# The identity held in the factor of the DeltaNet's solves: one VectorE operation for each Newton residual

## The chip, the cores and the metric

One Trainium2 chip, one core of it. The metric is the device time of one launch in microseconds (us); the figures compared are medians of several launches. TensorE (PE in the profile, PEld its weight loads), VectorE (DVE), ScalarE (ACT), GpSimd (POOL) and the DMA queues of SyncE (SP) each work through a list of instructions in order, and wait for one another by semaphores.

## The reference

One decoder layer for 512 tokens of width 1024: norm, an input projection whose columns feed three groups of heads, an output projection, and an MLP. Only the gated DeltaNet (6 heads of 64, chunks of 64 tokens) bears on the change:

```python
decay = jnp.exp(jnp.where(causal, gc[..., :, None] - gc[..., None, :], -jnp.inf))
L = jnp.where(strict, jnp.einsum('bhncd,bhnsd->bhncs', k_beta, k) * decay, 0.0)
A = jnp.eye(C, dtype=f32) + L
u = lax.linalg.triangular_solve(A, v * beta[..., None], left_side=True, lower=True, unit_diagonal=True)
w = lax.linalg.triangular_solve(A, k_beta * jnp.exp(gc)[..., None], left_side=True, lower=True, unit_diagonal=True)
...
def step(S, xs):
    v_new = u_i - jnp.einsum('bhcd,bhde->bhce', w_i, S)
    o = jnp.einsum('bhcd,bhde->bhce', qd_i, S) + jnp.einsum('bhcs,bhse->bhce', qk_i, v_new)
    S = S * gl_i[..., None, None] + jnp.einsum('bhcd,bhce->bhde', kd_i, v_new)
    return S, o
```

## The kernel before

The kernel inverts A = I + L for each chunk. Tokens lie in 4 tiles of 128 (two chunks each), and `gdn_solve(i)` does tile i for all six heads at once: a 128x384 tile holds six 64x64 blocks on each half of the partitions, and `sysmm` (its matmuls are all on L809) multiplies them block by block, 12 steps of two 64x64 matmuls.

A solve first doubles an approximate inverse in float16 (T16 and its transpose TT16, six rounds on L834 to L846), then corrects it by Newton steps in float32. X is the approximation (a copy of T16, made by GpSimd on L857). `residual()` forms r = I - X - L X: IX = I - X on L852, and R = IX - L X on L854, where L X is a product in PSUM of the transposed factor LT and X. Then X += T r (L860), the transpose TT1 is corrected the same way (L863), a second residual follows, and the last correction (L870) is written over LT as d["TT"], the inverse's transpose. L874 multiplies it with k. `gdn_prep_k` makes LT (`decayed`, L755) and its negative float16 copy L16 (L777).

The solves run two by two: tiles 0 and 1, then 2 and 3 (`solves`). `gdn_step` (L889, L893, L897, L906, L909, L914) is one step of the scan over chunks; its steps 4 to 8 need the second pair of solves. `gdn_out` (L928 to L938) normalizes a tile's outputs. All of that shares the engines with the input projections of the other heads (`proj_tok`, L434: 128x256 matmuls against hi and lo halves of the weights; L559 and L547 belong to the key and query heads that these projections feed, L148 and L683 copy their results out), with the compression MLP (`compress_half`, L597, L608, L639), and behind the last projection with the attention (L1072 to L1149) and the output projection (L142 to L144 on the tiles hwo, lwo). A projection of `proj_tok` holds two of three PSUM banks (pm), so its second half waits until the projection before has been read out of the bank that it takes over.

The order on each engine isn't written by hand. `side_by_side` interleaves generators, and then a scheduler places all instructions by its own model of their times: the context is opened with `schedule_with_timeline_sim=True`. So a change of a few instructions can move many others.

Of the kernel before, what the change touches and what calls it, by code (L numbers as in the profile page):

```python
# [16 lines left out]
ALU = mybir.AluOpType  # L17
# [4 lines left out]
T = 512  # L22
# [15 lines left out]
def trunk_kernel(ctx, tc, x, norm_mix, w_in, conv_w, a_log, dt_bias, gdn_norm, nsa_q_norm, nsa_k_norm,  # L38
                 cmp_pos, cmp_w1, cmp_w2, pool_w, pool_scale, w_out, norm_ffn, w_ffn1, w_ffn2, out):
    nc = tc.nc  # L40
    V, S, G, PE, SY = nc.vector, nc.scalar, nc.gpsimd, nc.tensor, nc.sync
# [31 lines left out]
    def ctile(shape, dt, name):  # L73
        return cst.tile(shape, dt, tag=name, name=name)
# [201 lines left out]
    id2 = ctile([P, 64], F32, "id2")  # L276
# [4 lines left out]
    for p in range(2):  # L281
        h = slice(64 * p, 64 * p + 64)
# [84 lines left out]
    for m in range(6):  # L367
        n = 1 << m
        G.memset(lvf[:, m], 0.0)
        for p in range(2):  # L370
            h = slice(64 * p, 64 * p + 64)
# [5 lines left out]
    for p in range(2):  # L377
        h = slice(64 * p, 64 * p + 64)
# [337 lines left out]
    gt = gte.enter_context(pool("gt", 1))  # L716
    GB = dict(kT=2, D1=2, LT=4, QK=4, qdT=4, tmp=3, gls=2, vn=2, S=3, L16=4)
    for a in range(2):
        GB.update({f"X{a}": 1, f"IX{a}": 1, f"TT1{a}": 1, f"T{a}": 4, f"R{a}": 2})

    def bch(r):
        return r.unsqueeze(2).to_broadcast([P, H, HD])
# [1 line left out]
    def bs(m):  # L724
        return m.unsqueeze(1).to_broadcast([P, 6, 64])

    def w1t(shape, name, tag=None, dt=F32):
        tag = tag or name
        pl_ = gs if tag in ("LT", "QK", "qdT", "gls", "vn", "S", "tmp") else gt
        return pl_.tile(shape, dt, tag=tag, name=nm(name), bufs=GB[tag])  # L730

    def hcol(s_):

        return 2 * (s_ % 3) + s_ // 3

    def v6(ps):
        return ps[:, 0:384].rearrange("p (s c) -> p s c", s=6)

    def head_T(src):

        ps = pp_()
        for j in range(3):
            PE.transpose(ps[:, ts(j, P)], src[:, 2 * j:2 * j + 2, :].rearrange("p a d -> p (a d)"), ident)
        return ps[:, 0:384].rearrange("p (j a t) -> p j a t", j=3, a=2)

    def decayed(dst, kT, qT, dec):

        for hp in range(2):
            kk = pp_()
            for j in range(3):  # L750
                for p in range(2):
                    PE.matmul(kk[halves[p], ts(j, 64)], kT[halves[hp], j, p], qT[halves[hp], j, p], start=True, stop=True)
            yield 0.3
            ss = slice(3 * hp, 3 * hp + 3)
            V.tensor_tensor(dst[:, ss], kk[:, 0:192].rearrange("p (s c) -> p s c", s=3), dec[:, ss], ALU.mult)  # L755

    def gdn_prep_k(i):

        gU = w1t([P, 2, 3, 64], "gU", "tmp")
        gi = g[:, i].rearrange("p (j a) -> p a j", a=2)  # L760
        for hp in range(2):
            G.tensor_tensor(gU[:, hp], gi[:, hp].unsqueeze(2).to_broadcast([P, 3, 64]),
                            le64.unsqueeze(1).to_broadcast([P, 3, 64]), ALU.mult)
        de = pp_()
        PE.matmul(de[:, 0:384], sgt, gU.rearrange("p a j c -> p (a j c)"), start=True, stop=False, skip_group_check=True)
        PE.matmul(de[:, 0:384], identb, bs(nm64), start=False, stop=True, skip_group_check=True)
        yield 0.9
        D1, LT = w1t([P, 6, 64], "D1"), w1t([P, 6, 64], "LT")
        D0 = w1t([P, 6, 64], "D0", "tmp")
        S.activation(D1, v6(de), AF.Exp)  # L770
        V.tensor_tensor(D0, D1, bs(lt64), ALU.mult)
        kT = w1t([P, 3, 2, 64], "kT")
        S.copy(kT, head_T(kr[:, i]))
        yield 0.4
        yield from decayed(LT, kT, kT, D0)
        L16 = w1t([P, 6, 64], "L16", "L16", F16)
        V.tensor_scalar(L16, LT, -1.0, None, ALU.mult)  # L777
        grp[i] = dict(kT=kT, D1=D1, LT=LT, L16=L16)
        have.add(("k", i))

# [23 lines left out]
    def sysmm(pb, lhsT, rhs):  # L804

        ps = pb()
        for s_ in range(6):
            for p in range(2):
                PE.matmul(ps[halves[p], ts(s_, 64)], lhsT(halves[p], s_), rhs(halves[p], s_), start=True, stop=True)  # L809
        return v6(ps)  # L810

    def at(t):
        return lambda h, s_: t[h, s_]
# [8 lines left out]
    def gdn_solve(i):  # L822


        d = grp[i]
        LT = d["LT"]
        ln = i % 2
        pb = (pga, pgb)[ln]

        def tl(name, tag, dt=F32):  # L830
            return w1t([P, 6, 64], name, f"{tag}{ln}", dt)

        T16, TT16 = WI[ln][0], WI[ln][6]
        V.copy_predicated(TT16, bs(lv[:, 6]), d["L16"])  # L834
        for m in range(6):
            W = WI[ln][m]
            yp = sysmm(pb, at(d["L16"]), (lambda h, s_: id16[h]) if m == 0 else at(T16))
            V.copy_predicated(W, bs(lv[:, m]), yp)
            yield 0.33
            if m:  # L840
                nt = tl("T16", "T", F16)
                S.copy(nt, sysmm(pb, at(TT16), at(W)))
                yield 0.33
                tt = tl("TT16", "T", F16)
                S.copy(tt, sysmm(pb, at(W), at(TT16)))
                T16, TT16 = nt, tt  # L846
                yield 0.33

        X, IX = tl("X", "X"), tl("IX", "IX")

        def residual():
            V.tensor_tensor(IX, bs(id2), X, ALU.subtract)  # L852
            r = tl("R", "R", F16)
            V.tensor_tensor(r, IX, sysmm(pb, lambda h, s_: LT[h, s_], at(X)), ALU.subtract)  # L854
            return r

        G.tensor_copy(X, T16)  # L857
        r = residual()
        yield 0.8
        V.tensor_tensor(X, sysmm(pb, at(TT16), at(r)), X, ALU.add)  # L860
        yield 0.33
        TT1 = tl("TT1", "TT1")
        V.tensor_tensor(TT1, sysmm(pb, at(r), at(TT16)), TT16, ALU.add)  # L863
        t16 = tl("TT16", "T", F16)
        S.copy(t16, TT1)
        yield 0.33
        r = residual()
        yield 0.8
        d["TT"] = LT
        V.tensor_tensor(d["TT"], sysmm(pb, at(r), at(t16)), TT1, ALU.add)  # L870
        yield 0.33
        yield from until(("q", i))
        ke = kr[:, i]
        S.mul(ke, sysmm(pb, lambda h, s_: ke[h, hcol(s_)], at(d["TT"])), -1.0)  # L874
        yield 0.8
# [120 lines left out]
    def until(*names):  # L996
        while not have.issuperset(names):
            yield -1
# [11 lines left out]
    def solves():  # L1010
        for i in range(2):
            yield from gdn_prep_k(i)
        for ab in ((0, 1), (2, 3)):
            yield from until(*(("k", i) for i in ab))
            yield from in_turn(gdn_solve(i) for i in ab)
            have.add(ab)

    def preps():
        yield from until("q")
        for i in range(4):  # L1020
            if i == 2:
                yield from gdn_prep_k(2)
                yield from gdn_prep_k(3)
            yield from gdn_prep_q(i)
# [314 lines left out]
    for e in range(NE):  # L1339
# [40 lines left out]
        X, Y, Z = (0, 1), (2, 3), (6, 7)  # L1380
# [45 lines left out]
```

## Time and profile before

| what | value |
|---|---|
| median of 3 runs | 719.96 us (719.61 to 721.62) |
| the profiled execution's own time | 720.69 us |
| its span, first to last instruction | 718.7 us |
| PE busy | 695.0 us (97%) |
| DVE busy | 554.6 us (77%) |
| ACT busy | 385.0 us (54%) |
| POOL busy | 170.2 us (24%) |
| granted TensorE clock, mean | 0.997 of full |

Busy times are of single engines and overlap. [...] In rows of single instructions the first two numbers are the start and the duration in us, x counts instructions, and brackets give the idle time before the first of them with what ended it.

### The profile page before, as it was taken

The numbers are of one execution on the slowest core, as the hardware profiler recorded it, in microseconds if no ns is written. First come the engines' busy times: TensorE is split into PE (matmuls) and PEld (weight loads), VectorE is DVE, ScalarE is ACT, GpSimd is POOL, SyncE is SP. The second block draws the span as 40 slices with busy tenths as digits, with TensorE's granted clock in tenths as the row PEclk, the third lists the DMA queues.
The fourth block names the chain that finished last, engine by engine and source line by source line (L and its number), as shares of the span: only waits on it lengthen the run. The fifth ranks groups of instructions, "written<-read, shape, count | busy, mean of one in ns | idle before, by whom it ended". The sixth has DMA issues, their size and how long they took to land.

```text
span 718.7 us, 13300 instructions
## 1 busy us (share of the span) xinstructions
PE 695.0 (97%) x5161; PEld 570.1 (79%) x5161; DVE 554.6 (77%) x1041; ACT 385.0 (54%) x768; POOL 170.2 (24%) x257
## 2 busy tenths in 40 slices
PE   8999999999979898999889999999999999999997
PEld 7888777888969776676679878888888888888885
DVE  6688998888786669877454997977968686796836
ACT  5465845665744558686643845444544544634430
POOL 6820023313112400000030330504032140504123
PEclk9999999999999999999999999999999999999999
DMA  6343213142301503220120153333051423312103
GB/s 223 97 132 88 76 44 90 31 119 65 105 3 32 234 2 93 85 87 2 59 88 2 59 176 127 108 102 132 10 167 59 131 103 118 118 36 85 57 0 117
DMA packets 49923, 62.20 MB, mean 87 GB/s; under 512 B 5495, under 2 KB 42565, under 8 KB 49861
## 3 DMA queue, kind: packets, MB, share of 16 engines
q1 hardware_dynamic: 48996, 61.16, 27.0%
q8 instruction: 40, 0.66, 0.4%
q10 hardware_dynamic: 864, 0.20, 0.1%
q14 instruction: 23, 0.18, 0.1%
HBM read 59.25 MB, written 2.10 MB: 85 GB/s over the span
## 4 chain that ended last, share of the span: by engine, by line
PE 80%; DVE 10%; ACT 3%; DMA 3%; issue 2%; POOL 0%; SPq 0%; DVEq 0%; ACTq 0%; POOLq 0%
PE ps L142 19%; PE ps L143 18%; PE ps L144 18%; PE ps L434 7%; PE ps L809 3%; PE ps L1149 2%; PE ps L260 2%; PE ps L597 1%; PE ps L1135 1%; DMA raw<-in_w_in_dram 1%; ACT P L1116 1%; DMA raw<-in_cmp_w_dram 1%; DVE lw L134 1%; DVE bl L1302 1%; PE ps L1110 1%
## 5 line engine op out<-in xcount | busy, mean ns | idle before, releaser
L143 PE MATMUL ps<-h2l,hw 128*128 128x512 f32 (+1 forms) x280 | 104.9, 375 | 0.2 <-DVE h2l L1273 0.2
L144 PE MATMUL ps<-h2h,lw 128*128 128x512 f32 (+1 forms) x280 | 104.5, 374 | 0.0
L142 PE MATMUL ps<-h2h,hw 128*128 128x512 f32 (+1 forms) x280 | 103.8, 374 | 0.0
L1309 POOL TENSOR_TENSOR al<-gF,ah 128x512 fp32r<-128x512 f32 x24 | 36.4, 1516 | 224.0 <-ACT ah L1308 184.6
L142 PE MATMUL ps<-bh,ah 128*128 128x512 f32 x224 | 88.4, 395 | 0.7 <-DVE x L1395 0.7
L143 PE MATMUL ps<-bl,ah 128*128 128x512 f32 x224 | 88.1, 393 | 0.0
L144 PE MATMUL ps<-bh,al 128*128 128x512 f32 x224 | 84.5, 393 | 0.0
L1395 DVE TENSOR_TENSOR x<-ps,x 128x512 f32<-128x512 f32 x112 | 72.7, 680 | 8.4 <-PE ps L144 8.4
L1302 DVE TENSOR_TENSOR bl<-w2r,bh 128x1024 fp32r<-128x1024 f32 x40 | 57.8, 1446 | 6.6 <-ACT bh L1301 6.6
L143 PEld LDWEIGHTS ps<-h2l,hw 128*128 128x128 f32 x280 | 52.6, 188 | 10.4 <-DVE h2l L1273 0.4
L144 PEld LDWEIGHTS ps<-h2h,lw 128*128 128x128 f32 x280 | 52.6, 188 | 10.0
L142 PEld LDWEIGHTS ps<-h2h,hw 128*128 128x128 f32 x280 | 52.3, 188 | 10.1
L1309 POOL TENSOR_TENSOR al<-gS,ah 128x512 fp32r<-128x512 f32 x32 | 53.8, 1698 | 22.1 <-ACT ah L1308 22.1
L1301 ACT CAST bh<-w2r 128x1024 fp32r<-128x1024 f32 x40 | 41.8, 1047 | 26.5 <-PE ps L144 26.0
L134 DVE TENSOR_TENSOR lo<-raw,hi 128x512 fp32r<-128x512 f32 (+1 forms) x76 | 43.0, 587 | 11.0 <-ACT hi L133 10.4
L133 ACT CAST hi<-raw 128x512 fp32r<-128x512 f32 (+1 forms) x76 | 37.4, 518 | 26.2 <-DMA raw<-in_w_in_dram 9.5
L142 PEld LDWEIGHTS ps<-bh,ah 128*128 128x128 f32 x224 | 42.1, 188 | 11.4 <-ACT ah L1308 0.9
L144 PEld LDWEIGHTS ps<-bh,al 128*128 128x128 f32 x224 | 42.1, 188 | 9.8
L143 PEld LDWEIGHTS ps<-bl,ah 128*128 128x128 f32 x224 | 42.1, 188 | 9.6
L134 DVE TENSOR_TENSOR lw<-raw,hw 128x1024 fp32r<-128x1024 f32 x32 | 41.2, 1321 | 5.8 <-ACT hw L133 5.7
L133 ACT CAST hw<-raw 128x1024 fp32r<-128x1024 f32 x32 | 32.2, 1046 | 25.0 <-PE ps L143 22.7
L1308 ACT CAST ah<-gS 128x512 fp32r<-128x512 f32 x32 | 19.7, 621 | 46.4 <-DVE gS L1377 24.4
(370 smaller groups left out, 1676.8 us busy)
## 6 DMA issues: line engine op xcount, KB each, us to landing
raw<-in_w_ffn_dram SPq DMA_DIRECT2D x32, 512.0 KB, 3.9
w2r<-in_w_ffn_dram SPq DMA_DIRECT2D x32, 512.0 KB, 4.6
raw<-in_w_in_dram SPq DMA_DIRECT2D x24, 256.0 KB, 3.0
raw<-in_w_in_dram SPq DMA_DIRECT2D x36, 128.0 KB, 2.5
x<-in_x_dram SPq DMA_DIRECT2D x8, 512.0 KB, 6.2
raw<-in_cmp_w_dram SPq DMA_DIRECT2D x32, 128.0 KB, 2.8
raw<-in_w_out_dram SPq DMA_DIRECT2D x8, 512.0 KB, 4.3
out_dram<-x SPq DMA_DIRECT2D x8, 256.0 KB, 2.0
```

What stands on the lines that cost most here:

```text
L133: {"A": S.copy, "V": V.tensor_copy, "G": G.tensor_copy}[e[0]](hi[:, k], r)
L134: {"V": V, "G": G}[e[1]].tensor_tensor(lo[:, k], r, f32v(hi[:, k]), ALU.subtract)
L142: PE.matmul(ps, ah, bh, start=start, stop=False, **kw)
L143: PE.matmul(ps, ah, bl, start=False, stop=False, **kw)
L144: PE.matmul(ps, al, bh, start=False, stop=stop, **kw)
L434: PE.matmul(ps[:, ts(i, 256)], a_[:, k, ts(2 * b + i, P)], w_, start=(k == 0 and n_ == 0 and i == 0), stop=(k == KC - 1 and n_ == 2 and i ...
L809: PE.matmul(ps[halves[p], ts(s_, 64)], lhsT(halves[p], s_), rhs(halves[p], s_), start=True, stop=True)
L1301: S.copy(hi, src)
L1302: V.tensor_tensor(lo, src, f32v(hi), ALU.subtract)
L1308: S.copy(hi, src)
L1309: G.tensor_tensor(lo, src, f32v(hi), ALU.subtract)
L1395: V.tensor_tensor(x2[i][:, cs], acc[bk, t_], x2[i][:, cs], ALU.add)
```

## The change

L852 and the tile IX go. In their place the identity id2 (a 64x64 identity in each block, read as a broadcast) is added to LT once for each tile, in `gdn_prep_k` behind L777, where L16 has already been taken from it. LT's diagonal was zero, so LT then holds the transpose of I + L, and the product in PSUM is X + L X; R = id2 - that product is one operation. The two IX tiles (128x384 float32, one for each of the pair) are no longer allocated. The product's matmuls are the same in number and shape.

```diff
-        GB.update({f"X{a}": 1, f"IX{a}": 1, f"TT1{a}": 1, f"T{a}": 4, f"R{a}": 2})
+        GB.update({f"X{a}": 1, f"TT1{a}": 1, f"T{a}": 4, f"R{a}": 2})
...
         L16 = w1t([P, 6, 64], "L16", "L16", F16)
         V.tensor_scalar(L16, LT, -1.0, None, ALU.mult)
+        V.tensor_tensor(LT, LT, bs(id2), ALU.add)
         grp[i] = dict(kT=kT, D1=D1, LT=LT, L16=L16)
...
-        X, IX = tl("X", "X"), tl("IX", "IX")
+        X = tl("X", "X")

         def residual():
-            V.tensor_tensor(IX, bs(id2), X, ALU.subtract)
             r = tl("R", "R", F16)
-            V.tensor_tensor(r, IX, sysmm(pb, lambda h, s_: LT[h, s_], at(X)), ALU.subtract)
+            V.tensor_tensor(r, bs(id2), sysmm(pb, lambda h, s_: LT[h, s_], at(X)), ALU.subtract)
             return r
```

On every engine the instructions are the same but for those on DVE (8 of L852 gone, 4 additions new), yet their order differs from the middle of the first solves on. In the changed program lines from 778 to 850 stand one higher (L809 is L810 there). The pieces below show three places.

**VectorE, the Newton steps of the second pair.** X_2785 and X_2815 before, X_2783 and X_2811 now, belong to tiles 2 and 3; R, IX and TT1 (shown as TT) likewise. qks, r and rs belong to a norm of the key heads, and ps_3824 before, ps_3816 now, is the bank that the second half of the next projection takes over when L547 has read it. Before:

```order
L852 TENSOR_TENSOR IX_2816<-id_148,X_2815 128x384
L111 SCALAR_TENSOR_TENSOR r_4016<-rs_4021,r_4016 128x4
L863 TENSOR_TENSOR TT_2908<-ps_2909,TT_2767 128x384
L547 TENSOR_TENSOR qks_4014<-ps_3824,r_4016 128x2x128
L854 TENSOR_TENSOR R_2929<-IX_2786,ps_2930 128x384
```

and in the changed program:

```order
L547 TENSOR_TENSOR qks_4006<-ps_3816,r_4008 128x2x128
L613 SCALAR_TENSOR_TENSOR hh_3960<-ht_3961,hh_3960 128x128
L839 COPY_PREDICATED W_570<-lv,ps_2656 128x384
...
L854 TENSOR_TENSOR R_2785<-id_148,ps_2786 128x384
L111 SCALAR_TENSOR_TENSOR r_4032<-rs_4037,r_4032 128x4
...
L860 TENSOR_TENSOR X_2783<-ps_2831,X_2783 128x384
```

L547, which releases the bank, stood behind seven operations of the Newton steps on X, R and TT and four on IX; now it stands ahead of all of them.

**TensorE, the same place.** L809 and L810 are the solves' products, L434 the projection into the bank named above (ps_4085 before, ps_4077 now). Before:

```order
L809 MATMUL ps_2790<-X_2785,LT_1375 64x64 x12
...
L639 MATMUL ps_2707<-w_3962,hh_3968 32x64 x12
L809 MATMUL ps_2820<-X_2815,LT_1410 64x64 x12
...
L809 MATMUL ps_2837<-R_2789,TT_2749 64x64
...
L809 MATMUL ps_2930<-X_2785,LT_1375 64x64 x12
L809 MATMUL ps_2949<-X_2815,LT_1410 64x64 x12
L434 MATMUL ps_4085<-hi_4086,hTh 128x256
```

and in the changed program:

```order
L810 MATMUL ps_2786<-X_2783,LT_1377 64x64 x12
L559 MATMUL ps_4054<-ident,X_4002 128x128
...
L434 MATMUL ps_4077<-hi_4078,hTl 128x256
...
L810 MATMUL ps_2831<-R_2785,TT_2747 64x64
L434 MATMUL ps_4077<-lo_4079,hTh 128x256
...
L810 MATMUL ps_2814<-X_2811,LT_1413 64x64 x12
L810 MATMUL ps_2878<-TT_2747,R_2785 64x64
```

Before, from the first residual's product to the second residuals' products no projection stands between them, only the 12 rows of L639; now 11 rows of L434 stand between the first residual's product and the next product of the solves (TT16 with W), and 21 between the first correction and the residual of the other tile, and such runs go on to the end of the solves.

**TensorE, the end of the projections.** L434 is the last projection, L1072 the first of the attention, L889 and L914 steps of the scan (ps_3327 is step 6 before; ps_3239 and ps_3279 are steps 4 and 5 now). Before:

```order
L434 MATMUL ps_4224<-hi_4283,hTl 128x256
L1072 MATMUL ps_4513<-KCT,XT_3564 128x64 x2
L1072 MATMUL ps_4513<-KCT,XT_3571 128x64 x4
L889 MATMUL ps_3327<-vb,LT_1410 64x64
L889 MATMUL ps_3327<-vb,LT_1375 64x64
```

and in the changed program:

```order
L434 MATMUL ps_4216<-hi_4275,hTl 128x256
L1072 MATMUL ps_4505<-KCT,XT_3556 128x64
L914 MATMUL ps_3239<-S_3209,qdT_1450 64x64
...
L1072 MATMUL ps_4505<-KCT,XT_3563 128x64 x4
L1072 MATMUL ps_4496<-KCT,XT_3549 128x64 x4
L1072 MATMUL ps_4496<-KCT,XT_3556 128x64 x2
L889 MATMUL ps_3279<-vb,LT_1377 64x64 x6
```

Of the steps that need the second pair, 4 and 5 stood ahead of the projections' end before; now the end of step 4 and all of 5 to 8 stand behind it, among the attention. On VectorE's list L932 of the last tile moves from place 590 to 609; on TensorE's the fourth L936 stands 17 rows ahead of the third head's L1170, 33 before. Behind the middle of the attention the orders on TensorE have met again.

## Rows read from the trace of the kernel before

**Rows 1.** The page: busy time of the engines.

```profile
PE 695.0 (97%) x5161; PEld 570.1 (79%) x5161; DVE 554.6 (77%) x1041; ACT 385.0 (54%) x768; POOL 170.2 (24%) x257
```

**Rows 2.** Windows: busy time by stage (x instructions), granted clock, DMA.

```profile
core 0: us, PE busy (x) PEld busy (x) DVE busy (x) ACT busy (x) POOL busy (x), PEclk, DMA share, GB/s
150.00:170.00 20.00, 19.68 (x404) 17.15 (x402) 16.68 (x50) 11.78 (x32) 2.17 (x5) 1.00 0.32 94
199.80:209.62 9.82, 6.09 (x181) 5.20 (x174) 8.82 (x30) 4.45 (x17) 1.01 (x2) 1.00 0.01 2
209.62:213.30 3.68, 3.68 (x53) 3.56 (x54) 2.57 (x8) 1.88 (x5) 1.74 (x4) 0.54 0.00 0
213.30:238.70 25.40, 25.40 (x341) 23.82 (x341) 14.96 (x43) 9.35 (x22) 7.73 (x15) 1.00 0.08 23
238.70:250.00 11.30, 9.06 (x119) 6.95 (x118) 9.78 (x29) 8.19 (x21) 4.21 (x7) 1.00 0.86 334
250.00:275.00 25.00, 25.00 (x181) 19.01 (x180) 18.76 (x51) 14.67 (x39) 1.02 (x1) 1.00 0.06 20
275.00:300.00 25.00, 21.95 (x126) 15.80 (x124) 23.50 (x67) 20.67 (x56) 1.01 (x1) 1.00 0.34 109
```

**Rows 3.** Timeline of PE, the end of the second pair.

```profile
202.35 0.92 PE L809 MATMUL ps<-X,LT 64*64 64x64 f32 x24 [0.41 <-ACT TT L845]
...
203.38 1.14 PE L639 MATMUL ps<-w,hh 128*32 128x64 f32 x24
204.96 0.92 PE L809 MATMUL ps<-X,LT 64*64 64x64 f32 x24 [0.44 <-ACT TT L845]
...
207.41 0.38 PE L809 MATMUL ps<-R,TT 64*64 64x64 f16 x12 [1.34 <-DVE R L854]
...
209.08 0.38 PE L809 MATMUL ps<-TT,R 64*64 64x64 f16 x12 [0.76 <-DVE X L860]
209.62 2.71 PE L809 MATMUL ps<-X,LT 64*64 64x64 f32 x48 [0.16 <-DVE TT L863]
...
216.42 1.61 PE L809 MATMUL ps<-LT,kr 64*64 64x64 f32 x48
```

**Rows 4.** Timeline of DVE, the same stretch.

```profile
205.08 0.54 DVE L852 TENSOR_TENSOR IX<-id,X 128x384 f32<-128x384 f32 x1
...
205.93 0.17 DVE L103 TENSOR_SCALAR r<-ss 128x4 int32<-128x4 int32 x1
...
206.81 0.55 DVE L854 TENSOR_TENSOR R<-IX,ps 128x384 f16<-128x384 f32 x1
...
207.93 0.56 DVE L852 TENSOR_TENSOR IX<-id,X 128x384 f32<-128x384 f32 x1
...
210.49 0.41 DVE L547 TENSOR_TENSOR qks<-ps,r 128x256 f32<-128x256 f32 x1
```

**Rows 5.** Lines L852 and L771: durations (ns min/median/max).

```profile
L852 DVE TENSOR_TENSOR IX<-id,X x8: 541/548/557, 146.6 to 209.5; 128x384 f32<-128x384 f32 x8
L771 DVE TENSOR_TENSOR D<-D,lt x4: 546/554/559, 55.8 to 127.3; 128x384 f32<-128x384 f32 x4
```

**Rows 6.** The chain that ended last: one run of projections.

```profile
225.61 3.19 PE ps L434 x25
```

**Rows 7.** Lines on PE, 238.7 to 300 us, by what was waited for.

```profile
L1110 PE MATMUL ps<-XT,XT 128*128 128x256 f32 (+3 forms) x28 | 10.3, 367 | 2.3 <-ACT P L1116 2.3
...
L1095 PE MATMUL ps<-ident,pc 128*96 128x128 f32 x4 | 0.6, 282 | 1.1 <-DVE pc L1091 1.1
```

**Rows 8.** Timeline: the last tile of the scan and of gdn_out.

```profile
270.43 0.54 DVE L929 TENSOR_REDUCE ss<-sq 128x6 f32<-128x384 f32 x1
285.65 0.55 DVE L932 TENSOR_TENSOR vb<-vb,r 128x384 f32<-128x384 f32 x1
...
286.34 1.01 POOL L933 TENSOR_TENSOR vb<-vb,zt 128x384 f32<-128x384 f32 x1 [32.30 <-DVE vb L932]
...
295.16 0.52 PE L936 MATMUL ps<-ident,vb 128*128 128x128 f32 x3 [0.18 <-DVE yTl L148]
```

## The prediction

> **What bounds the kernel now.** The page's first part comes first: PE is busy 695.0 of 718.7 us, DVE 554.6 [rows 1]. PE leaves 718.7 - 695.0 = 23.7 us idle in the whole span, and no edit on DVE can gain more than PE's idle time plus what PE loses to a low clock. So the second view is the windows, to see where near the change PE is idle or slow [rows 2]. The first pair's Newton steps lie in 150 to 170 us, under projections and compression: PE is busy 19.68 of 20.00 us there. The second pair's end is different. From 199.80 to 209.62 us PE is busy 6.09 of 9.82, so 3.73 us are idle, and from 209.62 to 213.30 it is busy throughout but at a granted clock of 0.54, which is nearly all of it at the lower of its two levels. Then PE is full to 238.7 us. In the attention 2.24 us of 11.30 and 3.05 of 25.00 are idle again.
>
> The third view is the timeline of PE in the poor stretch [rows 3]. Nothing but the solves' own small products and the compression's last ones (L639) stands there. The longest wait is 1.34 us for R of L854, another is 0.76 us for X of L860. The timeline of DVE shows why those are late [rows 4]: DVE is busy 8.82 of the 9.82 us [rows 2] and works off its queue in order. Between IX at 205.08 and R at 206.81 stand the first steps of a small rsqrt chain (L103 at 205.93 and on); IX at 207.93 stands directly behind the first tile's X and in front of the second's. The projection that could fill PE needs a bank that L547 frees, and L547 runs only at 210.49, behind all of that. So the hole is made by two queues that are interleaved badly, not by the Newton steps' length alone.
>
> **The change part by part.**
>
> *Operations.* Eight IX operations of 0.548 us go, four additions come; L771 is the nearest row for them (float32, same shape, one operand a broadcast): 0.554 us [rows 5]. DVE saves 8 x 0.548 - 4 x 0.554 = 2.17 us. R reads the broadcast identity where it read IX; L852 itself reads that broadcast at 0.548, so I take no change for R. The additions stand in front of the four solves' first mask operation (L834) and delay each by 0.55 us, at a time when PE has other work; without that cover it would be 4 x 0.55 = 2.2 us. On PE no instruction is added or removed. If nothing moved, the direct gain would be the IX operations on the chain of the poor stretch: four of them, 2.2 us, of which the part that turns into PE's waiting is at most the waits behind them (R 1.34, X 0.76 and the 0.16 before TT1's product [rows 3] give about 2.1).
>
> *The order.* This is the larger part, and it is told from the pieces of the two lists in the section on the change. L547 now stands in front of the second pair's residuals on DVE, so the bank is free, and PE's list has 11 and 21 projections between the products that waited for R and X. In a plain run 25 of them take 3.19 us on the chain that ended last [rows 6], 0.128 each, so 11 are 1.4 us and 21 are 2.7 us of cover. What must be covered is one DVE operation of 0.55 us and what is queued in front of it, which was 1.26 us at the first R of the poor stretch (205.55, where IX gave DVE free, to 206.81). So most of the 3.73 us should go.
>
> *The clock.* With the hole goes the slow stretch behind it: at a clock of 0.54, 3.68 us do the work of 3.68 x 0.54 = 1.99 us, so 1.69 us are lost. A direct check: 48 float32 products of 64x64 take 2.71 us at 209.62, and the same number at 216.42, at full clock, takes 1.61 [rows 3]; that alone is 1.10 us. [...]
>
> *What stays.* The new order also has two tight places: two products in a row that both need fresh masks (W) from DVE, and the last residual of tile 3. The first pair's stretch, which is covered in the same manner, still idles 20.00 - 19.68 = 0.32 us for two tiles' Newton steps [rows 2]. The bounds of what stays are 0 and the whole 3.73; I take 0.7, twice that row, since the new order's runs of projections are broken into more pieces than a plain one.
>
> *The attention.* The end of step 4 and steps 5 to 8 of the scan now stand among the attention instead of 4 and 5 ahead of it. PE's work is only moved. It can fill idle time there (5.29 us between 238.7 and 300 [rows 2], mostly waits for exponentials of L1116, 2.3 us, and for L1091, 1.1 us [rows 7]), or make DVE and ACT later, since DVE is busy 23.50 of the 25.00 us from 275 on [rows 2]. DVE's share of what is moved is small: about two steps of two operations, none longer than a 128x384 operation, so at most 4 x 0.55 = 2.2 us, as much as the change saves on DVE. I take 0, with bounds of 2 us either way, the idle time of 238.7 to 250 on the one side and those 2.2 us on the other.
>
> *The sum.* -3.73 - 1.69 + 0.7 + 0 = -4.7 us against the profiled execution: 720.69 - 4.7 = 716.0. That execution lies 0.73 us above the median, so against 719.96 it is 715.3 us.
>
> **The rivals.**
>
> *No change.* The hole is filled but the time isn't kept: either PE still waits (for masks, or for the DVE queue, which now has four residues of weights, L134, to do between the Newton steps), or the attention gives it back. For it speaks that DVE is nearly full in both stretches, 8.82 of 9.82 and 23.50 of 25.00 us. Against it: DVE is busy only 14.96 of 25.40 us in between [rows 2], and this is the stretch that the solves' end now shares. [...] The time by this rival: 719.96, within 2.2 either way.
>
> *Only the direct gain.* The new order brings nothing, and only the IX operations on the chain count, with the slow clock staying: 719.96 - 2.1 = 717.9. It lies on the border of what can be told apart.
>
> *Slower: the scan's end becomes late.* The last tile's `gdn_out` takes 270.43 to 285.65 on DVE, because its small operations are queued among the softmax's, then GpSimd until 287.35, and PE transposes the result at 295.16: 7.8 us of slack [rows 8]. In the new order the last scan step stands later against the attention, and on DVE the last L932 comes 19 places further down, while PE's last transpose moves by 16 of PE's rows only. At 23.50 us for 67 operations, 0.35 us each [rows 2], that is 6.7 us: the slack is nearly used up. If queueing is worse than this mean, PE stops at that transpose with the attention queued behind it. It turns the sign when that wait exceeds the 4.7 us gained, which is from 7.8 + 4.7 = 12.5 us of delay on. With each of the 19 places at twice the mean the delay is 13.3 us, and if in steps 5 to 8 of the scan each of two DVE operations is held up by one more of the mean, 4 x 2 x 0.35 = 2.8 us come to it: 13.3 + 2.8 - 7.8 = 8.3 us of waiting, and 719.96 + 8.3 - 4.7 = 723.6. That needs all of it to be late at once.
>
> **How the numbers follow.** A measurement of this kernel tells differences of about 0.3%, 2.2 us, from none. The forecast with its own spread has 0.66; the direct gain alone 0.08, half of it below the border; no change 0.16; slower 0.10. That gives faster 0.70, same 0.20, slower 0.10. The likeliest case's own range is 712.5 (all of 5.42 gained, and 2 more in the attention) to 717.8. The range for 8 in 10 goes up into the no-change case: 712.3 to 720.3, which leaves out the upper half of no change and the slower case above, and a little below.
>
> **What would show it.** In the changed kernel's windows the stretch between the compression's last product and the last projection should show PE busy in more than 95% and a clock of 1.00; the waits for R and X should be under 0.5 us together; the last projection should end some 7 to 8 us earlier than 238.7, because of the 4.7 us and of the scan's products that went behind it; the fourth L936 should wait less than 1 us. From 300 us on all stages should be equal, moved by one offset. I am wrong if PE's waits for DVE at the solves remain above 2 us, if the clock still falls there, or if the transposes of `gdn_out` or L1110 wait longer than before by as much as was gained.

## The result: 1.15% slower

The changed kernel takes 728.92 us (727.08 to 730.33, 4 runs) beside 719.97 (719.61 to 721.62, 4 runs) for the kernel before: the ratio is 1.0115, 95% interval 1.0098 to 1.0133. Its profiled execution took 727.69 us, with a span of 725.9, 7.2 more than that of before. The medians lie 8.95 us apart, the two profiled executions 7.0: the changed kernel's two longer executions (730.16 and 730.33) had a mean granted clock of 0.988 and 0.986, the two shorter ones 0.991. The prediction, 715.3 with a range up to 720.3, is wrong, and on the other side.

The page's first part, beside [rows 1]:

```profile
PE 700.5 (97%) x5161; PEld 574.2 (79%) x5161; DVE 554.7 (76%) x1037; ACT 384.9 (53%) x768; POOL 171.0 (24%) x257
```

VectorE's busy time is that of before, and PE is 5.5 us longer busy with the same 5161 products. In the changed kernel's trace the projections' products (L434, 128x256) are 415 to 452 ns long on the mean from 178.2 to 183.4 us, at a granted clock of 0.50, and 286 to 289 from 184 to 236 us, at 1.00, so this points at the clock. The windows, beside [rows 2]:

```profile
150.00:170.00 20.00, 19.72 (x404) 17.01 (x401) 16.77 (x50) 13.30 (x36) 2.19 (x5) 1.00 0.40 110
170.00:175.00 5.00, 4.11 (x98) 3.54 (x98) 4.72 (x22) 1.78 (x6) 1.64 (x4) 1.00 0.02 6
175.00:178.17 3.17, 0.44 (x20) 0.33 (x16) 1.69 (x4) 1.24 (x4) 2.17 (x5) 0.80 0.00 0
178.17:184.00 5.83, 5.83 (x56) 5.13 (x56) 1.38 (x3) 3.77 (x10) 0.65 (x1) 0.52 0.19 46
204.00:236.50 32.50, 31.92 (x522) 30.04 (x522) 19.31 (x54) 12.64 (x33) 11.25 (x20) 1.00 0.07 19
236.50:250.00 13.50, 12.70 (x156) 10.10 (x155) 11.94 (x38) 9.41 (x26) 3.29 (x4) 1.00 0.80 312
250.00:275.00 25.00, 25.00 (x230) 19.40 (x229) 19.17 (x57) 15.19 (x41) 3.29 (x4) 1.00 0.00 1
275.00:300.00 25.00, 20.49 (x113) 14.79 (x111) 22.37 (x68) 18.75 (x50) 2.05 (x1) 0.93 0.27 85
```

The poor stretch at the second pair's end is gone: from 204 us to the last projection PE is busy 31.92 of 32.50 us at full clock. But at the second pair's *start* there is a new one: 175 to 178.17 us has 0.44 us of work, and the 5.83 us behind it run at a clock of 0.52. (In slices of 0.2 us the clock of both traces is 1.00 or 0.50, but for 2 slices of before and 6 of the changed kernel at the edges of slow stretches.) The timeline of PE shows the wait:

```profile
173.74 0.38 PE L810 MATMUL ps<-W,TT 64*64 64x64 f16 x12 [0.90 <-DVE W L839]
...
175.04 0.40 PE L810 MATMUL ps<-T,L 64*64 64x64 f16 x10
178.17 0.53 PE L810 MATMUL ps<-TT,W 64*64 64x64 f16 x12 [2.73 <-ACT T L843]
178.63 0.58 PE L597 MATMUL ps<-hi,fs 128*128 128x256 f32 x1
```

PE waits 2.73 us for T of L843. ScalarE's timeline shows what that stands behind:

```profile
172.93 0.47 ACT L846 CAST TT<-ps 128x384 f16<-128x384 f32 x1
176.93 0.81 ACT L554 CAST X<-qks 128x256 fp32r<-128x256 f32 x2 [3.53 <-POOL qks L550]
177.65 0.47 ACT L843 CAST T<-ps 128x384 f16<-128x384 f32 x1
178.02 0.27 ACT L633 CAST KCT<-ps 128x128 fp32r<-128x128 f32 x1
```

The casts of L554 wait 3.53 us for GpSimd's qks (L550), which needs L547 from VectorE, and VectorE reaches that only at the end of a chain of small operations:

```profile
175.00 0.17 DVE L111 SCALAR_TENSOR_TENSOR r<-rs,r 128x8 f32<-128x8 f32 x1
175.20 0.37 DVE L546 TENSOR_SCALAR r<-r 128x4 f32<-128x4 f32 x1
175.60 0.69 DVE L547 TENSOR_TENSOR qks<-ps,r 128x512 f32<-128x512 f32 x1
176.21 0.55 DVE L839 CAST_PREDICATED W<-lv,ps 128x384 f16<-128x384 uint16 x1
```

It is the picture of [rows 4] again, a small rsqrt chain and L547 among the solves' work, 30 us earlier and with ScalarE's queue as the second link. What covered this stretch before were projections. The rows of L434 alone, of before and then of the changed kernel:

```profile
170.00:190.00 20.00, 9.31 (x67) 8.19 (x65) 1.00 0.41 106
190.00:210.00 20.00, 3.65 (x24) 3.13 (x24) 0.99 0.06 17
```

```profile
170.00:190.00 20.00, 5.70 (x31) 4.70 (x29) 0.83 0.24 61
190.00:210.00 20.00, 10.58 (x72) 9.39 (x73) 1.00 0.22 62
```

From 170 to 190 us 31 projections run where 67 did, and from 190 to 210 us 72 where 24 did: the cover of the old hole is missing at the new one.

Two windows for each kernel divide the 7 us: 60 us to the attention's first product (L1072), and from there to the first L1268, the first product behind the attention. Of before, then of the changed kernel:

```profile
60.00:238.70 178.70, 173.55 (x2514) 150.19 (x2512) 147.81 (x395) 102.12 (x250) 38.69 (x60) 0.99 0.24 63
238.70:370.16 131.46, 121.65 (x752) 89.15 (x750) 97.89 (x244) 85.99 (x213) 10.24 (x22) 1.00 0.22 77
```

```profile
60.00:236.50 176.50, 171.25 (x2428) 148.05 (x2427) 143.78 (x376) 100.46 (x245) 37.06 (x59) 0.98 0.24 64
236.50:377.13 140.63, 128.44 (x836) 94.64 (x834) 100.41 (x259) 87.85 (x218) 12.65 (x22) 0.98 0.21 72
281.50:287.00 5.50, 5.12 (x21) 3.65 (x21) 5.05 (x16) 5.17 (x16) 0.00 (x0) 0.69 0.29 97
361.00:366.00 5.00, 4.97 (x14) 3.50 (x15) 1.39 (x2) 1.19 (x2) 0.00 (x0) 0.66 0.00 0
```

| | idle PE, before and after | lost to the clock | length without both |
|---|---|---|---|
| to L1072 | 5.15 and 5.25 | 1.69 and 2.80 | 171.86 and 168.45 |
| attention | 9.81 and 12.19 | 0 and 3.41 | 121.65 and 125.03 |

Idle time is length less busy time. The clock's loss is the length of each slow stretch times what its clock lacks, where PE is busy: 5.83 x 0.48 = 2.80 behind the new hole (the lower clock in the hole itself falls on time that is already counted as idle), and 5.50 x 0.31 + 5.00 x 0.34 = 3.41 at 281.5 and 361 us. The last column shows the scan's products that moved (86 fewer rows in the first window, 84 more in the second). The differences are +0.10 +1.11 -3.41 and +2.38 +3.41 +3.38. The moved work cancels, and 6.97 us are left, 4.52 of them the clock's and 2.48 idle time. From there on both kernels run alike (offset 6.97 at L1268, 7.2 at the end).

### The profile page after: what moved, and what is told of

Its sections match the earlier page's. It is cut to its first block, busy times and chain, and to the rows that moved or that the text cites. A ratio compares the mean times of both kernels' runs of the same rounds, so it can differ in the third digit from the quotient of the medians.

```text
span 725.9 us, 13295 instructions
## 1 busy us (share of the span) xinstructions
PE 700.5 (97%) x5161; PEld 574.2 (79%) x5161; DVE 554.7 (76%) x1037; ACT 384.9 (53%) x768; POOL 171.0 (24%) x257
## 4 chain that ended last, share of the span: by engine, by line
PE 80%; DVE 9%; ACT 5%; DMA 3%; issue 2%; SPq 0%; POOL 0%; DVEq 0%; ACTq 0%; POOLq 0%
PE ps L143 19%; PE ps L142 19%; PE ps L144 19%; PE ps L434 6%; PE ps L810 3%; PE ps L597 2%; PE ps L260 2%; PE ps L1149 2%; DMA raw<-in_w_ffn_dram 2%; DMA raw<-in_w_in_dram 1%; PE ps L1135 1%; PE ps L1110 1%; DVE lw L134 1%; ACT P L1116 1%; PE ps L1268 1%
```

## Experiments

Two theories. **Order**: the scheduler's new order of the queues makes the time, and the operations little of it. **Work**: the operations themselves (additions ahead of the solves, a residual that reads a broadcast) cost it. Where an experiment holds an order, its kernel gets this function and a table of each engine's instructions, which is called behind the kernel's body:

```diff
+def _follow(tc, nc, order):
...
+    for e, text in order.items():
...
+        row = [per[e][k] for k in struct.unpack(f"<{len(raw) // 2}H", raw)]
+        for a, b in zip(row, row[1:]):
+            tc.add_manual_dep(b, a.name, nosync, reason="order")
```

No kernel was run with its own order held, so what holding costs by itself isn't measured. That it is little is argued from the fifth experiment, which is held and still faster than before.

**First and second: operations and order crossed.** The new operations in the old order, and the old ones in the new order.

> The changed kernel's operations, with every engine's queue held in the order of the kernel before; each addition stands directly behind the negation of L777, and nothing is left out. If the order decides, this is the time of before less what the missing IX operations gave on the chain: 717.9 to 720.0 us, with the hole of 199.8 to 209.6 us shortened by at most 2.1. If the operations themselves decide (the additions ahead of the solves' first masks, the residual's broadcast operand), it is near the changed kernel's 728.9.

> The operations of the kernel before (IX in, no additions), with every engine's queue held in the order of the changed kernel; each IX stands directly ahead of its residual. If the order decides, this is the changed kernel's time plus at most the eight IX operations: 728.9 to 731. If the operations decide, it is near 720.

Measured: 723.37 us for the first, 1.0024 of before (1.0009 to 1.0040), and 727.71 for the second, 1.0086 (1.0070 to 1.0103), with 721.04 for before beside them. With the old operations the new order loses 0.86% of the changed kernel's 1.15%, and its trace has the same wait of 2.7 us for T. So the order is most of the loss, though the time lies 1.2 us below the range that this theory had; the rest, 0.29%, is at the edge of the two intervals and not explained. But the first was not the small gain that the order theory wanted: by its ratio it lost 1.7 us. Its trace shows where, ScalarE's and then PE's rows:

```profile
115.51 0.62 ACT L133 CAST hi<-raw 128x512 fp32r<-128x512 f32 x1 [3.58 <-DMA raw<-in_w_in_dram]
```

```profile
117.35 1.82 PE L671 MATMUL ps<-pM,PW 128*128 128x512 f32 x2 [2.43 <-issue]
```

A weight's transfer is late: its cast starts at 115.51, in the fifth experiment at 113.23. Its residue on VectorE follows at 116.38, behind that the pooling's last L668 at 117.09, and PE's L671 waits 2.43 us and starts right after it (the view names no releaser). Two additions stand at 85 and 97 us, and from 80 to 118 us VectorE has no gap in which to catch up (37.51 of 38.00 us busy). The DMA queue's own waits from 108 to 114 us (total, times, longest) show what the transfer waits for:

```profile
SPq L126 <- DVE lo L134: 5.7, 1, 5.7
SPq L126 <- DVE pw L660: 1.9, 1, 1.9
```

The issues of the weights' transfers (L126) wait for VectorE, as in the fifth experiment, but VectorE is 2.0 us later here, and the first of these issues starts at 110.91, in the fifth at 108.91.

**Third: the additions on GpSimd.**

```diff
-        V.tensor_tensor(LT, LT, bs(id2), ALU.add)
+        G.tensor_tensor(LT, LT, bs(id2), ALU.add)
```

> The change with its four additions on GpSimd instead of VectorE; the scheduler then gives a third order, in which PE's list differs from before's at about a third as many places as the changed kernel's does. If the order decides, the time has no reason to be the changed kernel's: 716 to 724, and idle PE time stands at other places. If the missing IX operations or the residual's broadcast operand cost the time, it is 727 to 730.

Measured: 723.05, 1.0032 (1.0020 to 1.0044). Neither the changed kernel's time nor a gain; a hole at 115 us again, which the eleventh explains.

**Fourth and sixth: the new hole.** In the changed kernel's own order one cast, then two, go ahead on ScalarE:

```diff
+L843 CAST T
+L633 CAST KCT
 L554 CAST X
 L554 CAST X
-L843 CAST T
-L633 CAST KCT
```

> The changed kernel in its own order but for one move: on ScalarE the cast to T (L843), which stood behind two casts of L554 that wait for GpSimd, goes ahead of these. If the hole of 175 to 178 us is that place in the queue, PE's wait of 2.73 us for T falls below 0.7 and the clock stays at 1.00, which gives back 2.0 of idle time and some 2.7 of work at half clock: 724.2. If the next late thing takes its place (the mask W behind L547 on VectorE, which ends at 176.8), the wait is 1.6 us, the clock falls all the same, and the time is 727 to 728.

> The changed kernel in its own order, with the two casts on ScalarE that were seen to be waited for in turn (T of L843 and KCT of L633) both ahead of the two casts of L554 that wait for GpSimd. If that place in ScalarE's queue makes the hole at 175 to 178 us, its 2.3 to 2.7 us and the slow clock behind it (5.5 us at half clock, 2.75 us of work) go: 722.5 to 724.5. If the mask behind L547 on VectorE is the real limit, PE still waits about 1.6 us and the time is 727 to 728.

Measured: 727.75 with T alone, 1.0095 (1.0078 to 1.0111), and 726.51 with both, 1.0084 (1.0069 to 1.0099). PE's waits from 165 to 185 us, of the fourth and of the sixth:

```profile
PE ps L597 <- ACT KCT L633: 2.3, 1, 2.3
```

```profile
PE ps L559 <- POOL X L555: 2.0, 2, 1.6
```

Each time the next user of the same late chain takes over the wait. The fourth's time is that of its second case, by another waiter than named; the sixth is 2 us above its first case. The queue place was only the first link, and what is late is L547. The sixth also has no slow stretch in the attention (its mean clock from L1072 to L1268 is 1.00), yet its attention is only 1.39 us shorter than the changed kernel's, 139.24 us: of the 3.41 us of slow clock 2.02 came back, as 0.70 us more idle time and 1.33 more busy time for the same products.

**Fifth: the additions in gaps.** The first experiment's kernel, with each addition moved down on VectorE to a place where that trace shows it waiting.

```diff
 L777 TENSOR_SCALAR L
-L778 TENSOR_TENSOR LT
...
+L778 TENSOR_TENSOR LT
 L674 SCALAR_TENSOR_TENSOR yTl
```

> The changed kernel's operations in the order of before, as in the first experiment, but with the four additions moved on VectorE to places where it waited for something else in that experiment's trace: in front of L674 (1.43 us of waiting), L771 (1.16), the mask of the second pair's third step (0.80) and the residue behind it (1.16). If the first experiment lost its 3.7 us at 115 to 119 us because VectorE has no gap there and two additions made a weight's transfer late, this goes and the missing IX operations are left as a gain: 718.9 to 720.6, beside 721.04 of before. If the loss has another cause (the residual reading the broadcast identity, the missing IX), it stays at about 723.4.

Measured: 719.19, 0.9981 (0.9972 to 0.9990), beside 720.51. By the ratios the place of the additions is worth 0.43%, 3.1 us, and the operations by themselves gain 1.4 (0.7 to 2.0). It is the one version of the whole computation that beats both kernels. The stretch of [rows 2] in it:

```profile
199.80:209.62 9.82, 6.89 (x213) 6.10 (x213) 8.19 (x30) 5.27 (x18) 1.32 (x3) 1.00 0.01 2
209.62:213.30 3.68, 2.96 (x51) 2.45 (x48) 2.51 (x12) 0.88 (x3) 1.43 (x4) 1.00 0.02 4
```

PE's idle time is about that of before (3.65 in 13.50 us beside 3.73), but its longest waits are shorter (1.17 for R, 0.37 for X, beside 1.34 and 0.76), and the clock stays at 1.00. The gain is the slow stretch of 1.69 us, not the hole.

**Seventh and eighth: the attention.** The changed kernel's order up to L1072 and the rest in the order of before; the eighth with the sixth's edit as well.

> The changed kernel's operations in its own order up to the attention's first product (L1072), and what is left over from there in the order of before. If the attention's order costs the 6 us that the traces show between there and L1268 (6.97 us later than before at its end, about 1 at its start), the time is 721.5 to 723. If the hole in the second pair is all of the loss, it stays at 727 to 729.

> The two edits together: the changed kernel's order up to L1072 with T and KCT ahead of the casts of L554, and the order of before from there. If both are causes and add up, 716.5 to 719, faster than before (721.04); if they overlap (the second pair's delay is only handed on to the attention), 720 to 723.

Measured: 728.87, 1.0115 (1.0100 to 1.0130), and 727.23, 1.0091 (1.0075 to 1.0108). The seventh has the time of its second case, but not for its reason, as the attention did become shorter; the eighth misses both of its cases. The windows of the seventh, from the last projection to L1072, and then to L1268:

```profile
236.16:243.69 7.53, 3.92 (x86) 3.34 (x85) 3.39 (x15) 1.15 (x3) 1.31 (x3) 0.79 0.74 250
243.69:377.57 133.88, 125.87 (x751) 93.25 (x750) 98.01 (x244) 86.56 (x215) 9.78 (x21) 0.96 0.19 61
```

The attention is 133.88 us long, nearly as before (131.46) and 6.7 less than in the changed kernel. But the scan's steps that the changed order had left over now stand alone in front of it, and cost 7.53 us, half of them idle, with a slow clock behind: 0.50 in each microsecond from 243 to 254 us.

**Ninth and tenth: the reverse.** The fifth's kernel up to the last compression product (L597), or up to L1072, and the rest in the changed kernel's order.

> The fifth experiment's kernel (new operations, order of before, additions in VectorE's gaps) up to the compression's last weight product (L597, at about 199 us), and what is left over from there in the changed kernel's order. So the hole of 199.8 to 209.6 us is filled with projections, without the hole at 175. If filling it is a gain that is kept, as the prediction had it, the time is 715.5 to 717. If the projections spent there are missing later, under the scan's steps, which then fall into the attention (114 of their products stand behind its first one in the changed kernel's order, 72 in that of before), PE is full to the last projection all the same, but the attention gives it back: 719 to 723.

> The fifth experiment's kernel up to the attention's first product (L1072), with 72 products of the scan's steps left over as in before, and the rest in the changed kernel's order. If the attention of the changed kernel loses its time by the scan's steps that were moved into it, the time is that of the fifth experiment, 719 to 720.5. If it loses it by its own order, whatever is left of the scan, 723 to 726.

Measured: 731.22, 1.0141 (1.0119 to 1.0162), and 729.89, 1.0119 (1.0096 to 1.0142). Both are slower than either theory had it. The ninth is no clean test of filling the hole: where the two orders meet PE waits 3.4 us for the compression's hid (L605), and the clock from 195 to 210 us is 0.71. The tenth answers its question, in its attention's window:

```profile
239.19:382.41 143.22, 129.07 (x752) 93.49 (x750) 98.31 (x244) 87.08 (x215) 11.33 (x22) 0.95 0.21 71
```

With only the scan products of before left over (the same 752 rows), the new order needs 143.22 us for the attention, where the fifth, with the same beginning, needs 131.26. So the moved scan isn't the cause; the order is. The 12 us are an upper figure: the profiled execution, 733.35, is the slowest of four and 3.5 above their median, and right behind the place where the two orders meet stands a slow stretch of some 3.3 us of loss that the changed kernel doesn't have there:

```profile
239.19:250.57 11.38, 9.09 (x36) 6.46 (x35) 7.60 (x16) 7.23 (x18) 2.24 (x4) 0.70 0.91 352
```

**Eleventh and twelfth: half of the change each,** ordered by the scheduler.

```diff
-            V.tensor_tensor(IX, bs(id2), X, ALU.subtract)
...
-            V.tensor_tensor(r, IX, sysmm(pb, lambda h, s_: LT[h, s_], at(X)), ALU.subtract)
+            V.tensor_tensor(r, bs(id2), sysmm(pb, lambda h, s_: LT[h, s_], at(X)), ALU.subtract)
```

```diff
         V.tensor_scalar(L16, LT, -1.0, None, ALU.mult)
+        V.tensor_tensor(w1t([P, 6, 64], "SP", f"IX{i % 2}"), LT, bs(id2), ALU.add)
```

> Half of the change: the eight IX operations go, the residual reads the broadcast identity, and there are no additions, so that the Newton steps refine with L instead of L + I and the output isn't the reference's. The scheduler gives the same order as with the additions on GpSimd (third experiment, 723.05). If that kernel lost its time to the additions at 85 and 97 us, which made VectorE late in a stretch without a gap, the hole at 115 to 120 us is gone and the time is 719 to 720.5. If the third order is slow by itself, about 723.

> The other half: the kernel before with four additions of L777's result and the identity into a spare tile that nothing reads, IX kept. The scheduler gives a fourth order, which leaves that of before at the same row of PE's list as the changed kernel does (334 rows into its third hundred of projections, at about 100 us) and then goes its own way. If the time is made by the order, it has no fixed relation to the four operations: anywhere from 719 to 730, and PE's idle time and what it loses to the slow clock explain the difference to before within 1.5 us. If the four operations cost by themselves what they cost in the first experiment, 723 to 725, with a hole at 115 to 120 us.

(The number in the last brackets is a slip: in the traces both leave the order of before behind PE's 586th row, at 99 us.) Measured: 718.99 for the removal, 0.9978 (0.9968 to 0.9988), and 739.86 for the additions, 1.0268 (1.0243 to 1.0294). The removal has the third experiment's order without its additions, and no hole at 115 us (PE is busy 10.00 us from 115 to 125, in the third 7.67), so those cost 0.54%, 3.9 us, on GpSimd too. VectorE is late there as well: the four multiplications of L529 at 99 us take 862 ns each in the third and 557 in the eleventh, of which the last section tells more. And four additions that nothing reads make the kernel 19 us slower, outside both ranges: PE idles 33.9 us in this span and 23.7 in that of before, and slow stretches lose 6.0 us of PE's busy time beside 1.7, together 14.5 of the 18.4 us between the spans (3.9 left, where the expectation allowed 1.5). What four additions cost with an order held is 4 us at most in the experiments above, so most of it is put down to the order; no kernel held this order without the additions.

## Why the prediction was wrong

**Operations.** Each operation was priced right: L778 takes 0.560 us, and 4.40 us of IX are gone. But VectorE's busy time did not fall by 2.17 us: it is 554.7 us beside 554.6, as other operations take 2.3 us longer in the new order (in the fifth, with the order of before, it falls to 553.0). "At a time when PE has other work" was not enough as cover. In the old order the additions stand where VectorE is full, and their place costs 3.1 us (first and fifth). That loss isn't in the changed kernel itself, which has no such hole at 115 us.

**The hole and its clock, -3.73 and -1.69.** The mechanism was right at its place: L547 earlier, projections between the Newton steps, PE full, clock at 1.00. Summed over the stage it gained nothing: 5.15 us idle before, 5.25 after, and in place of the slow stretch that lost 1.69 us another that lost 2.80. This is the first step that failed. I read the two orders only at the end of the second pair, where the hole of before was; they differ from about 100 us on, and at the second pair's start, where 36 projections fewer run from 170 to 190 us, the same collision appeared. The sign "PE above 95% from the compression's last product on" held (98%); it looked past the new hole. That the slow stretch goes with the hole's idle time was my estimate; no run shows that the one hangs on the other, and in the fifth the stretch is gone while PE still idles 3.65 us in the same 13.50.

**What stays, 0.7.** In the stretch that it was meant for, right: waits of 0.6 us from 204 us to the last projection, and none for R or X.

**The attention, 0 with bounds of 2.** The second step that failed, and the larger one: 9.17 us longer, 3.4 of it moved work, 2.4 idle and 3.4 the clock's. I had bounded it by VectorE's moved operations; the tenth shows, with the scan's work where it was before, that the order of the attention itself costs up to 12 us there, some 3 of them where the two orders meet. (The seventh's 6.7 us less contain the 3.4 of moved work, so they prove less.) Which rows of the order do it isn't settled: no single wait of PE between 238 and 300 us exceeds 1.2 us.

**The last projection** ends 2.2 us earlier, not 7 to 8: 3.4 of moved products less 1.2 lost.

**The rivals.** "Only the direct gain", 2.1, is what the operations are worth with the order held and the additions in gaps: 1.4. "No change" named the mechanism, the attention giving the time back, at too small a size. The slower one was right in sign and not in mechanism. The last tile, beside [rows 8]:

```profile
279.17 0.55 DVE L929 TENSOR_REDUCE ss<-sq 128x6 f32<-128x384 f32 x1 [0.93 <-ACT sq L928]
...
294.10 0.55 DVE L932 TENSOR_TENSOR vb<-vb,r 128x384 f32<-128x384 f32 x1
```

```profile
294.79 2.05 POOL L933 TENSOR_TENSOR vb<-vb,zt 128x384 f32<-128x384 f32 x1 [25.13 <-ACT yTh L147]
```

```profile
300.06 0.52 PE L936 MATMUL ps<-ident,vb 128*128 128x128 f32 x3 [1.07 <-DVE sm L1090]
```

L932 is 8.45 us later than before, L933 ends at 296.84, and the transposes wait 1.07 us: the slack shrank, but it held.

## What to carry to other kernels

Under a scheduler, cost an edit twice: the operations with the order held, here -1.4 us, and the order, of which the scheduler's four for nearly the same instructions span 719 to 740 us here. Read the difference of two orders from its first row to its last, and count idle time and slow clock over a whole stage: projections that cover one chain can be missing at another, as here, where 31 of them ran in place of 67. An operation added to an engine can delay what is queued behind it (the place of four additions was worth 3.1 us here), so put it where that engine waits.

## What was not expected of the hardware

Where VectorE and GpSimd work side by side, which of the two takes longer can change between two kernels that do the same there. VectorE's four multiplications of L529 run beside the first of GpSimd's two of L789, at 98 to 102 us. In the first experiment, and then in the fifth, where both come some 0.8 us earlier:

```profile
L529 DVE TENSOR_TENSOR qr<-qr,rsq 128x384 f32<-128x384 f32 x4 | 3.2, 866 | 0.0
```

```profile
L789 POOL TENSOR_TENSOR qd<-qr,egc 128x384 f32<-128x384 f32 x2 | 2.1, 1075 | 51.7 <-DVE qr L529 51.7
```

```profile
L529 DVE TENSOR_TENSOR qr<-qr,rsq 128x384 f32<-128x384 f32 x4 | 2.0, 550 | 0.0
```

```profile
L789 POOL TENSOR_TENSOR qd<-qr,egc 128x384 f32<-128x384 f32 x2 | 3.0, 1476 | 51.1 <-ACT hi L133 51.1
```

Beside the other run, VectorE pays 1.2 us in the first and GpSimd 0.8 in the fifth. The kernel before and the changed kernel have it as the fifth: 549 and 550 ns for L529, 1480 and 1562 for GpSimd's two (L788 before). Why one of the two is slower, and what decides which, isn't shown. It isn't the distance of the two, which is 0.70 and 0.69 us; the first L529 and the first L789 of the first experiment, then of the fifth:

```profile
98.77 3.23 DVE L529 TENSOR_TENSOR qr<-qr,rsq 128x384 f32<-128x384 f32 x4
99.47 1.01 POOL L789 TENSOR_TENSOR qd<-qr,egc 128x384 f32<-128x384 f32 x1 [51.69 <-DVE qr L529]
```

```profile
98.01 1.96 DVE L529 TENSOR_TENSOR qr<-qr,rsq 128x384 f32<-128x384 f32 x4
98.70 1.95 POOL L789 TENSOR_TENSOR qd<-qr,egc 128x384 f32<-128x384 f32 x1 [51.10 <-ACT hi L133]
```

This matters for the time. In the first experiment the slowed L529 took VectorE's delay against the fifth from 0.8 us to 2.0 (L502 behind L529 starts at 101.92 and 99.88), and the weights' transfer is issued late by the same 2.0 us. So more than half of that delay comes from the slowed L529 and not from the additions' own 0.56 us each. In the changed kernel, whose own order has additions at 86 and 97 us too, L529 takes 550 ns each and there is no hole at 115 us (PE is busy 9.23 of the 10 us from there on). Whether the first experiment would have its hole without the slowed L529 was not tested.
